# Chunk state update of a state-space layer: one fp32 product replaced by three passes over split operands

## The chip, the cores and the metric

The kernel runs on one core of one Trainium2 chip. The metric is the device time of one execution in microseconds (us). Three runs of the kernel before took 1937.16, 1936.15 and 1934.88 us; their median is 1936.15 us.

## What is computed

One decoder layer over 1024 positions of width 1024, in float32. `u = h @ w_in` feeds a Conformer branch (a gated unit, a causal depthwise convolution of 31 taps, a layer norm, a product), a Mamba-2 state-space branch and two gates; the gated sum goes through `w_o` and a layer norm, and a convolutional gated MLP follows. The change lies in the state-space branch. It works on chunks of 128 positions, for 4 groups of 8 heads (64 channels each) with a state of 128:

```python
xs = (x * dt[..., None])                       # positions x heads x channels
cb = jnp.einsum("bclgn,bcsgn->bcgls", cc, bc)
y_diag = jnp.einsum("bcgrls,bcsgrp->bclgrp", cb[:, :, :, None] * decay, xs)
decay_states = jnp.exp(a_cs[..., -1:] - a_cs)
states = jnp.einsum("bclgn,bcgrl,bclgrp->bcgrpn", bc, decay_states, xs)
...
    return d_c[..., None, None] * carry + s_c, carry     # scan over the chunks
...
y_off = jnp.einsum("bclgn,bcgrpn,bcgrl->bclgrp", cc, prev, jnp.exp(a_cs))
```

The product that the change touches is `states`: for one group and one chunk the transposed B (128 positions x 128 states) times the scaled x (128 positions x 512 channels).

## The kernel before

The sequence is worked in two halves of 512 positions, `mixers(0)` and `combine(0)`, then `mixers(1)` and `combine(1)`, then the MLP. Nearly all large products are made from operands that are split in two: a high part, the value rounded to the type `fp32r`, and a low part, the float32 value minus the high part. `mm3` (L187) then issues three TensorE passes of 128x512 into one bank of PSUM: high x high (L190), high x low (L191), low x high (L192). `project` (L194) calls it 8 times for a column block, so a block is 24 passes. ScalarE makes a weight's high part (L156), VectorE its low part (L161).

`mixers` runs over 4 groups. For each it projects columns, applies a convolution of 4 taps to B, C and x (`conv4`, L517), makes the gate (`z_gate`), the gated unit of two blocks of channels (`glu`, L540 to L542), then the chunks (`ssd_group`), and, at low priority, the 31 taps of two blocks of channels (`conv31`, L564), 30 VectorE instructions of 128x512 for each block. Per chunk `ssd_group` has on TensorE: 4 transposes of x and one of B (L614, L617), the product of B and C (L618), 8 small products with the masked decay `m` (L653), 8 with the carried state (L656, none in the first chunk) and, unless it is the last chunk of the sequence, the state product (L661). There are 16 chunks with a state product in the first half (4 groups x 4) and 12 in the second. On VectorE: the two scaled copies of x (L638, L643), the masked B and C product (L636), `m` times it (L648), the state update (L665, L668), the result (L671, L681). GpSimd multiplies `ce` by C (L632). The operands of the state product are plain float32: `xsd` (L643, read out of PSUM) and `bt` (L647, a ScalarE copy out of PSUM).

`combine` adds up the branches. The layer norm over the convolution's channels needs all 8 blocks: GpSimd sums them (L803), a product with a constant gives the mean (L808), VectorE subtracts (L810), ScalarE squares, GpSimd sums (L816), a second product (L820), a root and a reciprocal (L821, L822), a multiplication (L825), a SiLU (L826), and the split of the result `sT` (L206, L207). The products `w_co` of `sT` come after those of `w_gb` and `w_sp`, which do not need it.

The order on each engine is made when the program is built, by a scheduler that places instructions by priority and by what it takes to be ready. Each engine then works through its own list in order. SyncE issues most of the DMAs.

Of the kernel before, what the change touches and what calls it, by code (L numbers as in the profile page):

```python
# [8 lines left out]
F32 = mybir.dt.float32  # L9
F32R = mybir.dt.float32r  # L10
AF = mybir.ActivationFunctionType
ALU = mybir.AluOpType
# [4 lines left out]
P = 128  # L17
D = 1024
T = 1024
HALF = 512  # L20
# [41 lines left out]
def kernel(  # L62
# [124 lines left out]
    def mm3(ps, wa, xa, start, stop, more=False):  # L187


        TE.matmul(ps, wa(0), xa(0), start=start, stop=False, skip_group_check=more)  # L190
        TE.matmul(ps, wa(0), xa(1), start=False, stop=False, skip_group_check=more)  # L191
        TE.matmul(ps, wa(1), xa(0), start=False, stop=stop, skip_group_check=more)  # L192
# [337 lines left out]
    def glu(pl, hh, hT, i):  # L530
        pa, pg = bank(1), bank(1)
        wa = col_weights(hh, CT_A + i)
        project(pa, wa, hT)
        wg = col_weights(hh, CT_G + i)
        project(pg, wg, hT)
        v = (statep if i & 2 else pl).tile(
            [P, HALF + KC - 1], F32, tag="v", bufs=2, name=f"v{hh}_{i}"
        )
        s = pl.tile([P, HALF], F32, tag="sig", name=f"sig{hh}_{i}")
        A.activation(out=s, in_=pg, func=AF.Sigmoid)  # L540
        A.copy(v[:, : KC - 1], v_halo[:, i, :])
        V.tensor_mul(v[:, KC - 1 :], pa, s)  # L542
        if hh == 0:
            A.copy(v_halo[:, i, :], v[:, HALF:])
        return v
# [44 lines left out]
    def ssd_group(pl, hh, g, xT, BT, CT, zs):  # L590
        S = states[g]
        h8 = slice(8 * g, 8 * g + 8)

        def heads(t):
            return t.rearrange("p (h q) -> p h q", h=8)

        def per_head(t):
            return t.unsqueeze(2).to_broadcast([P, 8, HP])

        ssum = pl.tile([P, HALF], F32, tag="ssum", name=f"ssum{hh}_{g}")  # L600
        for c in range(4):
            nm = f"{hh}_{g}_{c}"
            cs = slice(c * P, (c + 1) * P)
            first = hh == 0 and c == 0
            last = hh == 1 and c == 3
            ab = pl.tile([P, 8, P], F32, tag="ab", name=f"ab{nm}")
            r = c * HEADS + 8 * g
            SY.dma_start(
                ab.rearrange("p h l -> p (h l)"),
                acs_scr[hh][r : r + 8, :].rearrange("h l -> (h l)").partition_broadcast(P),  # L610
            )
            px = bank(0)
            for i in range(4):
                TE.transpose(px[:, i * P : (i + 1) * P], xT[:, i, cs], ident)  # L614
            pb = bank(0)
            if not last:
                TE.transpose(pb[:, :P], BT[:, cs], ident)  # L617
            TE.matmul(pb[:, P : 2 * P], BT[:, cs], CT[:, cs], start=True, stop=True)  # L618
            m = pl.tile([P, 8, P], F32, tag="m", name=f"m{nm}")
            for h in range(8):  # L620
                A.activation(  # L621
                    out=m[:, h, :],
                    in_=ab[:, h, :],
                    func=AF.Relu,
                    scale=-1.0,
                    bias=acs[:, c, 8 * g + h : 8 * g + h + 1],
                )
            exps.append(A.activation(out=m, in_=m, func=AF.Exp, scale=-1.0))
            if not first:
                ce = pl.tile([P, 8, P], F32, tag="ce", name=f"ce{nm}")  # L630
                A.activation(out=ce, in_=ab, func=AF.Exp)  # L631
                G.tensor_tensor(  # L632
                    out=ce, in0=ce, in1=CT[:, cs].unsqueeze(1).to_broadcast([P, 8, P]), op=ALU.mult
                )
            cbm = pl.tile([P, P], F32, tag="cbm", name=f"cbm{nm}")
            V.tensor_mul(cbm, pb[:, P : 2 * P], upper)  # L636
            xs = pl.tile([P, HALF], F32, tag="xs", name=f"xs{nm}")
            V.tensor_tensor(  # L638
                out=heads(xs), in0=heads(px), in1=per_head(dts[0][:, c, h8]), op=ALU.mult
            )  # L640
            if not last:
                xsd = pl.tile([P, HALF], F32, tag="xsd", name=f"xsd{nm}")
                V.tensor_tensor(  # L643
                    out=heads(xsd), in0=heads(px), in1=per_head(dts[1][:, c, h8]), op=ALU.mult
                )
                bt = pl.tile([P, P], F32, tag="bt", name=f"bt{nm}")
                A.copy(bt, pb[:, :P])  # L647
            V.tensor_tensor(out=m, in0=m, in1=cbm.unsqueeze(1).to_broadcast([P, 8, P]), op=ALU.mult)  # L648
            py = bank(0)
            for i in range(4):  # L650
                pair = [(2 * i + k, py[k * HP : (k + 1) * HP, i * P : (i + 1) * P]) for k in (0, 1)]
                for h, o in pair:
                    TE.matmul(o, xs[:, h * HP : (h + 1) * HP], m[:, h, :], start=True, stop=first)  # L653
                if not first:
                    for h, o in pair:
                        TE.matmul(  # L656
                            o, S[:, h * HP : (h + 1) * HP], ce[:, h, :], start=False, stop=True
                        )
            if not last:
                pn = bank(0)  # L660
                TE.matmul(pn, bt, xsd, start=True, stop=True)  # L661
                if first:
                    V.tensor_copy(S, pn)
                else:
                    V.tensor_tensor(  # L665
                        out=heads(S), in0=heads(S), in1=per_head(edc[:, 1, c, h8]), op=ALU.mult
                    )
                    V.tensor_add(S, S, pn)  # L668
            for i in range(4):
                k = PC_SD + 4 * g + i  # L670
                skip = V.scalar_tensor_tensor(  # L671
                    out=xT[:, i, cs],
                    in0=xT[:, i, cs],
                    scalar=pc[:, k : k + 1],
                    in1=py[:, i * P : (i + 1) * P],
                    op0=ALU.mult,
                    op1=ALU.add,
                )
            while held and c == 0:
                issue_after(held.pop(), skip)  # L680
            V.tensor_mul(xT[:, :, cs], xT[:, :, cs], zs[:, :, cs])  # L681
            sq = pl.tile([P, 4, P], F32, tag="sq", name=f"sq{nm}")
            A.activation(out=sq, in_=xT[:, :, cs], func=AF.Square)
            V.tensor_add(sq[:, 0:2], sq[:, 0:2], sq[:, 2:4])
            V.tensor_add(ssum[:, cs], sq[:, 0], sq[:, 1])

        def scaled():
            rstd = pl.tile([P, HALF], F32, tag="rstd", name=f"rstd{hh}_{g}")
            rows = pl.tile([P, P], F32, tag="rows", name=f"rows{hh}_{g}")
            pv = bank(0)  # L690
            for j in range(4):
                TE.matmul(
                    pv[j * HEADS : (j + 1) * HEADS, :P],
                    ones[:, :HEADS],
                    ssum[:, j * P : (j + 1) * P],
                    start=True,
                    stop=True,
                    tile_position=(0, j * HEADS),
                )
            A.activation(out=rows, in_=pv[:, :P], func=AF.Sqrt, bias=eps, scale=1.0 / HALF)  # L700
            V.reciprocal(out=rows, in_=rows)
            scr = nrm_scr[hh * GROUPS + g]
            G.dma_start(scr, rows.rearrange("(j r) l -> j r l", j=4)[:, 0, :])
            G.dma_start(rstd, scr.rearrange("j l -> (j l)").partition_broadcast(P))
            for i in range(4):
                k = PC_NW + 4 * g + i
                by_row = V.scalar_tensor_tensor(
                    out=xT[:, i, :],
                    in0=xT[:, i, :],
                    scalar=pc[:, k : k + 1],  # L710
                    in1=rstd,
                    op0=ALU.mult,
                    op1=ALU.mult,
                )
                held.append(by_row)

        def parts(yT):
            ks = slice((g % 2) * 4, (g % 2) * 4 + 4)
            hi, lo = yT[:, 0, ks], yT[:, 1, ks]
            for n in (slice(0, 2), slice(2, 4)):  # L720
                A.copy(hi[:, n], xT[:, n])
                V.tensor_tensor(
                    out=lo[:, n], in0=xT[:, n], in1=hi[:, n].bitcast(F32), op=ALU.subtract
                )

        return scaled, parts
# [768 lines left out]
```

## Time and profile before

| of the profiled execution | |
|---|---|
| span | 1934.5 us (no other time of this execution is listed; the median of the runs is 1.6 us above it) |
| VectorE busy | 1600.7 us, 83% of the span |
| ScalarE busy | 1092.2 us, 56% |
| GpSimd busy | 216.7 us, 11% |
| share of the DMA engines, in the 40 slices | 0.3 to 0.7 |
| granted TensorE clock | 0.999 |
| state products L661 | 56 records (two for each of 28 products), from 108.1 to 1057.4 us |

The page gives busy time by engine, then the span in 40 slices, then the chain of work that ended last, then groups of instructions. A group of TensorE passes shows a mean of about 390 ns each, but the passes overlap: what one costs is read from the starts in the timeline, not from its duration. The same holds, less strongly, for VectorE.

### The profile page before, as it was taken

The numbers are of one execution on the slowest core, as the hardware profiler recorded it, in microseconds if no ns is written. First come the engines' busy times: TensorE is split into PE (matmuls) and PEld (weight loads), VectorE is DVE, ScalarE is ACT, GpSimd is POOL, SyncE is SP. The second block draws the span as 40 slices with busy tenths as digits, with TensorE's granted clock in tenths as the row PEclk, the third lists the DMA queues.
The fourth block names the chain that finished last, engine by engine and source line by source line (L and its number), as shares of the span: only waits on it lengthen the run. The fifth ranks groups of instructions, "written<-read, shape, count | busy, mean of one in ns | idle before, by whom it ended". The sixth has DMA issues, their size and how long they took to land.

```text
span 1934.5 us, 25807 instructions
## 1 busy us (share of the span) xinstructions
PE 1921.9 (99%) x9424; PEld 1570.4 (81%) x9424; DVE 1600.7 (83%) x2230; ACT 1092.2 (56%) x1641; POOL 216.7 (11%) x256
## 2 busy tenths in 40 slices
PE   9999999999999999999999999999999999999998
PEld 8888877788888788888888888888888888887886
DVE  7599999999897639899999546597788888888778
ACT  7576767753353366776765435365555555543544
POOL 1001010112300001111112140010000000122010
PEclk9999999999999999999999999999999999999999
DMA  6645555547456665656545644566455555479673
GB/s 231 219 169 200 172 201 185 167 160 267 135 183 228 207 208 176 211 177 211 177 162 166 219 143 135 182 241 225 163 171 185 178 185 185 161 276 355 198 250 115
DMA packets 127216, 376.27 MB, mean 195 GB/s; under 512 B 15184, under 2 KB 15728, under 8 KB 127088
## 3 DMA queue, kind: packets, MB, share of 16 engines
q1 hardware_dynamic: 107424, 318.48, 48.7%
q0 software_dynamic: 13184, 44.59, 6.5%
q10 hardware_dynamic: 6480, 11.55, 1.6%
q8 instruction: 74, 1.21, 0.3%
q14 instruction: 54, 0.44, 0.1%
HBM read 290.00 MB, written 84.56 MB: 194 GB/s over the span
## 4 chain that ended last, share of the span: by engine, by line
PE 86%; DVE 9%; DMA 3%; ACT 1%; issue 1%; SPq 0%; DVEq 0%; POOL 0%; ACTq 0%; POOLq 0%
PE acc L192 20%; PE acc L191 20%; PE acc L190 20%; PE sm L190 6%; PE sm L192 6%; PE sm L191 6%; DVE c L564 3%; DMA dr<-wdown 2%; PE sm L653 1%; PE sm L661 1%; PE sm L656 1%; DVE x L517 1%; PE acc L498 1%; DMA st_wo<-wo 1%; PE sm L614 1%
## 5 line engine op out<-in xcount | busy, mean ns | idle before, releaser
L192 PE MATMUL acc<-hT_h,w_c 128*128 128x512 f32 x1000 | 391.4, 392 | 0.0
L191 PE MATMUL acc<-hT_l,w_c 128*128 128x512 f32 x1000 | 391.1, 391 | 0.0
L190 PE MATMUL acc<-hT_h,w_c 128*128 128x512 f32 x1000 | 391.0, 391 | 0.0
L564 DVE SCALAR_TENSOR_TENSOR c<-v,pc,c 128x512 f32<-128x512 f32 x480 | 371.1, 798 | 7.0 <-ACT c L553 4.5
L190 PEld LDWEIGHTS acc<-hT_h,w_c 128*128 128x128 f32 x1000 | 187.8, 188 | 40.6 <-issue 1.9
L192 PEld LDWEIGHTS acc<-hT_h,w_c 128*128 128x128 f32 x1000 | 187.8, 188 | 40.4 <-issue 1.5
L191 PEld LDWEIGHTS acc<-hT_l,w_c 128*128 128x128 f32 x1000 | 187.8, 188 | 39.5 <-issue 1.1
L156 ACT CAST w_c<-st_c 128x1024 fp32r<-128x1024 f32 x128 | 133.8, 1046 | 111.4 <-PE acc L192 84.3
L632 POOL TENSOR_TENSOR ce<-ce,xbc 128x1024 f32<-128x1024 f32 x28 | 78.3, 2796 | 686.8 <-ACT ce L631 686.8
L1260 ACT CAST w_dn<-dr 128x1024 fp32r<-128x1024 f32 (+1 forms) x72 | 67.2, 942 | 76.7 <-DVE dr L1193 36.0
L190 PE MATMUL sm<-h1s,w_s 128*128 128x512 f32 x264 | 102.8, 389 | 0.5 <-ACT fuv L1103 0.5
L191 PE MATMUL sm<-h1s,w_s 128*128 128x512 f32 x264 | 102.7, 389 | 0.0
L192 PE MATMUL sm<-h1s,w_s 128*128 128x512 f32 x264 | 102.2, 389 | 0.0
L621 ACT ACTIVATE m<-ab,acs 128x128 f32<-128x128 f32 x256 | 78.4, 390 | 39.5 <-PE sm L653 37.8
L161 DVE TENSOR_TENSOR w_c<-st_c,w_c 128x1024 fp32r<-128x1024 f32 x62 | 76.7, 1237 | 17.5 <-ACT w_c L156 17.4
L1261 DVE TENSOR_TENSOR w_dn<-dr,w_dn 128x1024 fp32r<-128x1024 f32 (+1 forms) x72 | 77.6, 1084 | 6.3 <-ACT w_dn L1260 6.2
L517 DVE SCALAR_TENSOR_TENSOR x<-u,pc,x 128x512 f32<-128x512 f32 x96 | 78.0, 826 | 5.7 <-ACT x L515 5.6
L192 PE MATMUL acc<-h1b_h,w_ue 128*128 128x512 f32 x176 | 68.7, 395 | 0.3 <-DVE w_ue L161 0.3
L190 PE MATMUL acc<-h1b_h,w_ue 128*128 128x512 f32 x176 | 68.8, 391 | 0.0
L191 PE MATMUL acc<-h1b_l,w_ue 128*128 128x512 f32 x176 | 68.6, 390 | 0.0
L190 PE MATMUL sm<-h1b_h,w_s 128*128 128x512 f32 x176 | 68.5, 389 | 0.0
L191 PE MATMUL sm<-h1b_l,w_s 128*128 128x512 f32 x176 | 68.5, 389 | 0.0
(369 smaller groups left out, 4544.7 us busy)
## 6 DMA issues: line engine op xcount, KB each, us to landing
st_c<-wcol SPq DMA_DIRECT2D x128, 512.0 KB, 4.4
low_scr<-w_c SPq DMA_DIRECT2D x64, 512.0 KB, 2.9
w_c<-low_scr SPq DMA_DIRECT2D x64, 512.0 KB, 4.4
ab<-acs_scr SPq DMA_DIRECT2D x32, 512.0 KB, 4.2
dr<-wdown SPq DMA_DIRECT2D x55, 256.0 KB, 4.9
st_wo<-wo SPq DMA_DIRECT2D x24, 512.0 KB, 4.3
st_ue<-wup SPq DMA_DIRECT2D x22, 512.0 KB, 3.7
first_scr<-first ACTq DMA_DIRECT2D x44, 256.0 KB, 3.0
```

The lines of the kernel that those rows point to most:

```text
L156: casts.append(A.copy(w[:, 0, :], st))
L161: sub.tensor_tensor(out=w[:, 1, :], in0=st, in1=w[:, 0, :].bitcast(F32), op=ALU.subtract)
L190: TE.matmul(ps, wa(0), xa(0), start=start, stop=False, skip_group_check=more)
L191: TE.matmul(ps, wa(0), xa(1), start=False, stop=False, skip_group_check=more)
L192: TE.matmul(ps, wa(1), xa(0), start=False, stop=stop, skip_group_check=more)
L498: mm = TE.matmul(pss[o][:, ts], ws[o][:, i, k * P : (k + 1) * P], hT[:, j, k, ts], start=n == 0 and k == 0, stop=n == 2 and k == KD - 1,)
L517: V.scalar_tensor_tensor(out=o, in0=u[:, k : k + HALF], scalar=pc[:, wc + k : wc + k + 1], in1=o, op0=ALU.mult, op1=ALU.add,)
L564: V.scalar_tensor_tensor(out=accs[i], in0=v[:, k : k + HALF], scalar=pc[:, wc + k : wc + k + 1], in1=accs[i], op0=ALU.mult, op1=ALU.add,)
L621: A.activation(out=m[:, h, :], in_=ab[:, h, :], func=AF.Relu, scale=-1.0, bias=acs[:, c, 8 * g + h : 8 * g + h + 1],)
L632: G.tensor_tensor(out=ce, in0=ce, in1=CT[:, cs].unsqueeze(1).to_broadcast([P, 8, P]), op=ALU.mult)
L1260: A.copy(w[:, 0, cs], src)
L1261: V.tensor_tensor(out=w[:, 1, cs], in0=src, in1=w[:, 0, cs].bitcast(F32), op=ALU.subtract)
```

## The change

```diff
-        s = pl.tile([P, HALF], F32, tag="sig", name=f"sig{hh}_{i}")
+        s = pl.tile([P, HALF], F32, tag="ya", bufs=2, name=f"sig{hh}_{i}")
...
             if not last:
-                xsd = pl.tile([P, HALF], F32, tag="xsd", name=f"xsd{nm}")
+                xsd = pl.tile([P, 2, HALF], F32R, tag="xsd", name=f"xsd{nm}")
+                whole = pl.tile([P, HALF], F32, tag="whole", name=f"whole{nm}")
                 V.tensor_tensor(
-                    out=heads(xsd), in0=heads(px), in1=per_head(dts[1][:, c, h8]), op=ALU.mult
-                )
-                bt = pl.tile([P, P], F32, tag="bt", name=f"bt{nm}")
-                A.copy(bt, pb[:, :P])
+                    out=heads(whole), in0=heads(px), in1=per_head(dts[1][:, c, h8]), op=ALU.mult
+                )
+                bt = pl.tile([P, 2, P], F32R, tag="bt", name=f"bt{nm}")
+                for n, src in ((bt, pb[:, :P]), (xsd, whole)):
+                    A.copy(n[:, 0, :], src)
+                    V.tensor_tensor(
+                        out=n[:, 1, :], in0=src, in1=n[:, 0, :].bitcast(F32), op=ALU.subtract
+                    )
...
-                TE.matmul(pn, bt, xsd, start=True, stop=True)
+                mm3(pn, lambda i: bt[:, i, :], lambda i: xsd[:, i, :], True, True)
```

Both operands are split as everywhere else, and the state product becomes three `fp32r` passes. Per chunk the change adds one ScalarE cast of 128x512 (`bt`'s copy becomes a cast), two VectorE subtractions (128x512 with both inputs in SBUF, 128x128 with one in PSUM), and turns one TensorE product of two records into three passes. No DMA is added. The tile `sig` of the gated unit loses its own buffer and takes turns in the two buffers `ya` that the branch results and gates use. Behind L648 the lines of the changed kernel stand 5 higher.

The scheduler makes a new order from this. Three places matter below. The first is a chunk's state product on TensorE, here the second chunk of the last group in the first half (`bt0_3_1`; `sm` is a PSUM bank, `w_so` a weight). Before:

```order
L656 MATMUL sm127_3661<-ce0_3_1_3649,state3_108 64x128 x2
L661 MATMUL sm128_3678<-xsd0_3_1_3656,bt0_3_1_3658 128x512
L614 MATMUL sm129_3693<-ident_75,x4_0_3_3137 128x128 x4
L617 MATMUL sm130_3698<-ident_75,xbc0_19_3087 128x128
L618 MATMUL sm130_3698<-xbc0_23_3128,xbc0_19_3087 128x128
L190 MATMUL acc142_3985<-yT0_0_h_1916,w_so0_5_3982 128x512
```

Of the change, on the same engine at the same chunk:

```order
L661 MATMUL sm127_3743<-ce0_3_1_3727,state3_108 64x128 x2
L190 MATMUL sm128_3760<-xsd0_3_1_3734,bt0_3_1_3737 128x512
L191 MATMUL sm128_3760<-xsd0_3_1_3734,bt0_3_1_3737 128x512
L192 MATMUL sm128_3760<-xsd0_3_1_3734,bt0_3_1_3737 128x512
L614 MATMUL sm129_3777<-ident_75,x4_0_3_3209 128x128 x4
L617 MATMUL sm130_3782<-ident_75,xbc0_19_3159 128x128
```

The three passes stand where the one product stood, between the small products of the old state and the next chunk's transposes.

The second place is VectorE around the same chunk (`c0_4`, `c0_5` are taps of the long convolution, `w_so` a weight's low part). Before:

```order
L643 TENSOR_TENSOR xsd0_3_1_3656<-sm125_3631,wds_110 128x512
L636 TENSOR_TENSOR cbm0_3_1_3652<-sm126_3636,upper_83 128x128
L564 SCALAR_TENSOR_TENSOR c0_5_2991<-v0_5_2727,pc_99,c0_5_2991 128x512
L564 SCALAR_TENSOR_TENSOR c0_4_2989<-v0_4_2659,pc_99,c0_4_2989 128x512
L681 TENSOR_TENSOR x4_0_3_3137<-x4_0_3_3137,zs0_3_3298 128x4x128
L161 TENSOR_TENSOR w_so0_5_3982<-st_so0_5_3980,w_so0_5_3982 128x1024
L648 TENSOR_TENSOR m0_3_1_3639<-m0_3_1_3639,cbm0_3_1_3652 128x1024
L564 SCALAR_TENSOR_TENSOR c0_5_2991<-v0_5_2727,pc_99,c0_5_2991 128x512
```

Of the change, from the second scaled copy's end on:

```order
L686 TENSOR_TENSOR x4_0_3_3209<-x4_0_3_3209,zs0_3_3370 128x4x128
L564 SCALAR_TENSOR_TENSOR c0_5_3063<-v0_5_2775,pc_99,c0_5_3063 128x512
L650 TENSOR_TENSOR xsd0_3_1_3734<-whole0_3_1_3735,xsd0_3_1_3734 128x512
L653 TENSOR_TENSOR m0_3_1_3717<-m0_3_1_3717,cbm0_3_1_3730 128x1024
L161 TENSOR_TENSOR w_so0_5_4078<-st_so0_5_4076,w_so0_5_4078 128x1024
L650 TENSOR_TENSOR bt0_3_1_3737<-sm126_3714,bt0_3_1_3737 128x128
L564 SCALAR_TENSOR_TENSOR c0_4_3061<-v0_4_2707,pc_99,c0_4_3061 128x512
```

The subtractions (L650) stand next to the chunk's multiplication; taps of the convolution move behind them, so that the convolution ends later.

The third place is TensorE at the end of the first half's convolution branch, where the products of `sT` begin. Before (`w_sp0_7` is the last block that does not need `sT`):

```order
L192 MATMUL acc171_5029<-yT0_2_h_4079,w_sp0_7_5032 128x512
L190 MATMUL acc172_5065<-sT0_4862,w_co0_0_5068 128x512
L191 MATMUL acc172_5065<-sT0_4862,w_co0_0_5068 128x512
L192 MATMUL acc172_5065<-sT0_4862,w_co0_0_5068 128x512
L190 MATMUL acc172_5065<-sT0_4862,w_co0_0_5068 128x512
```

Of the change:

```order
L192 MATMUL acc171_5125<-yT0_2_h_4175,w_sp0_7_5128 128x512
L190 MATMUL acc172_5161<-sT0_4958,w_co0_0_5164 128x512
L190 MATMUL acc173_5197<-sT0_4958,w_co0_1_5200 128x512
L191 MATMUL acc172_5161<-sT0_4958,w_co0_0_5164 128x512
L192 MATMUL acc172_5161<-sT0_4958,w_co0_0_5164 128x512
L190 MATMUL acc172_5161<-sT0_4958,w_co0_0_5164 128x512
L191 MATMUL acc173_5197<-sT0_4958,w_co0_1_5200 128x512
```

Two blocks of `w_co` now take turns, three passes each. Ahead of this, the mean product L808 has moved from the end of block `w_sp0_2` to just before the last pass of `w_sp0_4` (three blocks and 23 passes later), and L820 from behind `w_sp0_4` to behind `w_gb0_7`, so that only 48 passes, not 120, stand between L820 and the first pass of `w_co`. In the second half both stand where they stood. In SyncE's list some stores of the convolution's results and some loads of the chunks' decay rows (L574, L608) change places with a weight's load or store; the MLP's order is the same on every engine.

## The prediction

> **What bounds the kernel now.** I read the page's head, its chain of work, the waits of TensorE, and then the busy time by stage.
>
> ```profile
> span 1934.5 us, 25807 instructions
> PE 1921.9 (99%) x9424; PEld 1570.4 (81%) x9424; DVE 1600.7 (83%) x2230; ACT 1092.2 (56%) x1641; POOL 216.7 (11%) x256
> ...
> PE 86%; DVE 9%; DMA 3%; ACT 1%; issue 1%; SPq 0%; DVEq 0%; POOL 0%; ACTq 0%; POOLq 0%
> ```
>
> TensorE is busy for all but 12.6 us of the span, and the chain is 86% TensorE. So TensorE's list sets the time, and every other engine matters only where it makes that list wait. Of the stages that the change touches, the longest wait of TensorE for VectorE is one row (what a row's brackets hold is its idle time and releaser):
>
> ```profile
> 982.82 0.44 PE L653 MATMUL sm<-m,xs 128*64 128x128 f32 x4 [0.60 <-DVE m L648]
> ```
>
> But VectorE has little room there. The windows show, for the first half's chunks, the layer norm behind them, and the second half's chunks, the stage's length and then each engine's busy time (PE, PEld, DVE, ACT, POOL):
>
> ```profile
> 107.00:510.00 403.00, 403.00 (x2133) 324.68 (x2133) 398.59 (x581) 257.50 (x432) 49.46 (x33) 1.00 0.54 186
> 510.00:562.00 52.00, 52.00 (x228) 42.35 (x226) 39.97 (x50) 33.62 (x46) 13.79 (x12) 1.00 0.49 167
> ...
> 736.00:1075.00 339.00, 338.40 (x1904) 274.51 (x1903) 324.32 (x509) 236.75 (x385) 47.24 (x21) 1.00 0.55 184
> ```
>
> VectorE idles 4.4 us in the first stage, 12.0 in the second, 14.7 in the third. It holds because most of its work, the long convolution, can be put off. That makes the question: what does TensorE save, and does the added VectorE work come out as a wait?
>
> **The product on TensorE.** I go by the starts in the timeline: a chunk now; the one place where small float32 products are followed by `fp32r` passes; one where passes are followed by transposes; and eight steps of the plain stream.
>
> ```profile
> 145.90 0.39 PE L656 MATMUL sm<-ce,state 128*64 128x128 f32 x4
> 146.22 1.13 PE L661 MATMUL sm<-xsd,bt 128*128 128x512 f32 x2
> 147.18 0.60 PE L614 MATMUL sm<-ident,x 128*128 128x128 f32 x4
> ...
> 797.91 0.39 PE L656 MATMUL sm<-ce,state 128*64 128x128 f32 x4
> 798.23 0.50 PE L191 MATMUL acc<-hT_l,w_c 128*128 128x512 f32 x1
> 798.56 0.40 PE L192 MATMUL acc<-hT_h,w_c 128*128 128x512 f32 x1
> 798.80 0.39 PE L190 MATMUL acc<-hT_h,w_c 128*128 128x512 f32 x1
> ...
> 96.03 0.40 PE L192 MATMUL acc<-hT_h,w_c 128*128 128x512 f32 x1
> 96.26 0.60 PE L614 MATMUL sm<-ident,x 128*128 128x128 f32 x4
> ...
> 560.18 0.39 PE L192 MATMUL acc<-yT_h,w_sp 128*128 128x512 f32 x1
> ...
> 562.00 0.39 PE L191 MATMUL acc<-sT,w_co 128*128 128x512 f32 x1
> ```
>
> A plain pass costs 1.82 / 8 = 0.2275 us. Now: the state product starts 0.32 us after the last group of L656 and holds TensorE for 147.18 - 146.22 = 0.96 us. Changed: the first pass also starts 0.32 us after L656 (797.91 to 798.23), costs 0.33 us (it follows float32 work), the second 0.24, the third 0.23 until the transposes: 0.80 us. **Saved: 0.16 us a chunk, 28 x 0.16 = 4.5 us.** In the first half's four last chunks no transposes follow, and the sum is the same within 0.02 us. The new order also breaks one more run of passes with four small products (L692); by the same rows entering and leaving costs about 0.1 us each more than a plain pass, so I add 0.3 us.
>
> The Trainium skill, FP8 and Floating Point Precision, TensorE Precision Notes, says that true float32 takes four passes through the array. The two records' 0.96 us agree: four plain passes are 0.91. By that rule alone the change saves one pass in four, 28 x 0.2275 = 6.4 us; the row at 798.23, with its dearer first pass, speaks for the smaller saving.
>
> **What is added.** For VectorE and ScalarE:
>
> ```profile
> 539.69 3.70 DVE L825 TENSOR_TENSOR cc<-cc,stats 128x512 f32<-128x512 f32 x6
> ...
> 152.89 0.28 DVE L636 TENSOR_TENSOR cbm<-sm,upper 128x128 f32<-128x128 f32 x1
> 153.09 1.50 DVE L517 SCALAR_TENSOR_TENSOR x<-u,pc,x 128x512 f32<-128x512 f32 x1
> ...
> 505.90 1.21 DVE L161 TENSOR_TENSOR w_gb<-st_gb,w_gb 128x1024 fp32r<-128x1024 f32 x1
> 507.03 1.21 DVE L161 TENSOR_TENSOR w_sp<-st_sp,w_sp 128x1024 fp32r<-128x1024 f32 x1
> ...
> L206 ACT CAST mixT_h<-mb 128x512 fp32r<-128x512 f32 x16 | 10.0, 623 | 13.4 <-DVE mb L874 13.4
> L540 ACT ACTIVATE sig<-acc 128x512 f32<-128x512 f32 x16 | 9.5, 597 | 0.1
> ACT w_c L156 <- PE acc L192: 84.3, 43, 5.5
> ```
>
> Six two-input instructions of 128x512 take 3.70 us, so one costs 0.60 from start to start (the last lasts 0.68); one of 128x128 costs 0.20; a weight's low part 1.13. The two subtractions thus cost VectorE 0.80 us a chunk: 12.8 us in the first half, 9.6 in the second, 22.4 in all. ScalarE gets 28 casts of about 0.6 us, 17 us; in the first stage it idles for 145 us, and its weight casts are early: they wait 43 times for TensorE to free a buffer. I cost them at nothing; should one stand too early in ScalarE's list, a weight cast queues behind it and TensorE waits for that, a few tenths each time. The new buffers of `sig` cost nothing: ScalarE idles 0.1 us in all before L540. SyncE's moved stores and loads each pass one weight transfer; I cost them at nothing too, with 0.2 us a place if the cover were gone.
>
> **Does the chunk wait for its operands?** One chunk, VectorE's `m` and TensorE's first product with it:
>
> ```profile
> 396.53 1.21 DVE L648 TENSOR_TENSOR m<-m,cbm 128x1024 f32<-128x1024 f32 x1
> ...
> 400.93 0.44 PE L653 MATMUL sm<-m,xs 128*64 128x128 f32 x4
> ```
>
> The margin is 400.93 - 397.74 = 3.2 us. I summed both lists, by such starts, up to this pair at all 16 chunks of the first half: the new order has VectorE between 2.5 us less and 2.9 us more ahead of `m`, TensorE between 2.2 less and 3.0 more ahead of L653, and the difference never eats more than 0.2 us of a margin. Taps were put behind the chunk in exchange for the splits. The low parts end at most 3.7 us behind `m`, the passes that need them start 1.2 to 2.2 us behind L653, so margins of 2 to 5 us cover them. In the second half the 9.6 us fall on 14.7 us of idle time, most of which is one wait that simply gets shorter:
>
> ```profile
> DVE v L542 <- ACT sig L540: 8.6, 2, 5.5
> ```
>
> I cost this at nothing; the 0.60 us wait at 982.82 may grow or go. **The put-off taps end later**, and here they meet a deadline, the mean over all channels. Last taps of the first half, GpSimd's last sum, the product:
>
> ```profile
> 502.45 1.54 DVE L564 SCALAR_TENSOR_TENSOR c<-v,pc,c 128x512 f32<-128x512 f32 x2
> 504.13 1.30 POOL L803 TENSOR_TENSOR stats<-stats,c 128x512 f32<-128x512 f32 x1 [10.09 <-DVE c L564]
> 510.38 1.02 PE L808 MATMUL sm<-stats,mean_w 128*128 128x512 f32 x2
> ```
>
> The margin is 510.38 - 505.43 = 4.95 us. In the new order VectorE has, ahead of the last tap, 16 splits (12.8), five more low parts (5.7) and six more two-input instructions (3.6): 22.1 us. TensorE has 95 more passes ahead of L808 (21.6) less the saving (2.6): 19.0 us. The margin shrinks to 4.95 + 19.0 - 22.1 = 1.9 us: no wait.
>
> Then the norm's chain, with only 48 passes to hide it instead of 120:
>
> ```profile
> 533.02 1.02 PE L820 MATMUL sm<-stats,mean_w 128*128 128x512 f32 x2
> 534.28 1.28 ACT L821 ACT_TABLE_LOAD   x1
> 535.58 0.69 ACT L821 ACTIVATE stats<-sm,eps 128x512 f32<-128x512 f32 x1
> 536.30 3.35 DVE L822 RECIPROCAL stats<-stats 128x512 f32<-128x512 f32 x1 [0.53 <-ACT stats L821]
> ```
>
> From L820 to the reciprocal are 3.3 us, of which a weight cast of 1.05 stands ahead of the table load; in the new order it is a sigmoid of 0.6 instead: 2.9. Then 3.35, eight multiplications (4.8), one more two-input instruction (0.6), a low part (1.1) and the first low part of `sT` (0.7): it is there 13.4 us after L820. TensorE comes to the pass that needs it after 0.5 for L820, 48 passes (10.9, and 0.4 more for the first, behind float32 work) and two high passes (0.5): 12.3. **A wait of 1.2 us**, between nothing and 4 if ScalarE's SiLUs come late as well. **The sum:** -4.5 + 0.3 + 1.2 = -3.0 us, a span of 1931.5; on the median of the runs **1933.1 us**.
>
> **The rivals.** (a) *Full saving*: the chain keeps up and the wait at 982.82 goes too: 1936.15 - 4.5 + 0.3 - 0.6 = 1931.3 us. For it: margins everywhere in the trace. Against: the two `w_co` blocks that take turns show a scheduler with nothing else left. If float32 costs are as the four-pass rule has them, 1929.8. (b) *VectorE falls behind*, slower. Place: the last tap of the first half, ahead of L808. Rows:
>
> ```profile
> 898.58 2.54 POOL L632 TENSOR_TENSOR ce<-ce,xbc 128x1024 f32<-128x1024 f32 x1 [11.25 <-ACT ce L631]
> ...
> 898.77 4.47 DVE L564 SCALAR_TENSOR_TENSOR c<-v,pc,c 128x512 f32<-128x512 f32 x3
> ```
>
> Beside a GpSimd instruction three taps took 4.47 us where three plain ones take about 2.0: 2.4 us lost. The new 128x512 subtraction reads two operands from SBUF, as taps do. If one in four of the first half's 16 splits is held so over what the taps lose already, that is 9.6 us; 1.9 are margin, 7.7 become waits: 1933.1 + 7.7 = 1940.8 us. It decides from 1.9 us of lateness, and makes the kernel slower by 0.2% from about 9. Against it: a held split takes the place of a held tap.
>
> The Trainium skill, SBUF — State Buffer, Who interferes with whom, says so too: a VectorE instruction with two SBUF inputs and a GpSimd one that reads SBUF lock each other out for a whole instruction. The row at 898.77 agrees.
>
> (c) *Nothing moves*: stray waits behind ScalarE's casts, some tenths at each of 28 chunks, eat the 3 us: about 1936.
>
> **How the numbers follow.** A measurement of this kernel tells about 0.2%, 3.9 us, from no change. The forecast and (c) stay within it: 0.45. (a), with the forecast's lower edge, is faster: 0.33, of which 0.05 for the four-pass figure. (b) is slower: 0.22. The range from 1929.5 (the largest saving) to 1940.5 (most of (b)) leaves out about 0.15.
>
> **What would show it.** Right: three passes of 0.80 us between L656 and L614; L653 with margins as now; L808 without a wait; one wait of 1 to 2 us at the first L191 of `sT`. Wrong: a wait of TensorE at L808 or at several chunks (b), a weight cast late behind `xsd`'s (c), or 0.2 us and more a chunk saved (a). The forecast also falls if the order costs time at a place where I summed nothing, such as `conv4` before the transposes.

## The result, and the profile after

The change makes the kernel slower. Four runs took 1944.15 to 1949.33 us, median **1945.94 us**, beside 1935.92 us for the kernel before on the same chip: a ratio of **1.0052, with a 95% interval of 1.0039 to 1.0065**, about 10 us. The forecast was 1933.1 us, 3 us faster, with a range from 1929.5 to 1940.5. One execution each of three experiments below (`h_late`, where it is the profiled one, `f2_after27`, `j_passes27`) was disturbed as a whole (2751 to 5621 us) and is left out.

The profiled execution of the changed kernel has a span of 1942.4 us, 7.9 us longer than the profile of before. Its page, head and chain of work:

```profile
span 1942.4 us, 25956 instructions
...
PE 1920.1 (99%) x9452; PEld 1575.8 (81%) x9452; DVE 1625.9 (84%) x2286; ACT 1102.8 (57%) x1666; POOL 216.8 (11%) x256
...
PE 72%; DVE 20%; DMA 3%; issue 2%; ACT 2%; DVEq 0%; POOL 0%; SPq 0%; ACTq 0%; POOLq 0%
```

TensorE is busy 1.8 us less than before (1921.9), but the span is longer: it idles 22 us instead of 13. In the chain VectorE's share has risen from 9% to 20% at TensorE's cost. VectorE's busy time grew by 25.2 us, about what the durations of its 56 added instructions come to (26.9). The rows of the waits view that name TensorE and that belong to the changed part (total, times, longest):

```profile
PE sm L658 <- DVE m L653: 5.2, 5, 1.7
PE acc L191 <- DVE sT L207: 2.1, 1, 2.1
PE sm L813 <- POOL stats L808: 2.0, 1, 2.0
...
PE acc L192 <- DVE w_sp L161: 1.4, 1, 1.4
...
PE acc L192 <- DVE w_gb L161: 0.4, 1, 0.4
```

Before, this list held one row, 0.6 us for `m`. (L653, L658, L808, L813 are the old L648, L653, L803, L808.) Now there are 11.1 us in nine waits, all made by VectorE: the sum `stats` that GpSimd hands over was itself waiting for VectorE's last tap. The product itself is not at fault. One chunk of the first half in TensorE's timeline:

```profile
149.61 0.39 PE L661 MATMUL sm<-ce,state 128*64 128x128 f32 x4
149.92 0.50 PE L190 MATMUL sm<-xsd,bt 128*128 128x512 f32 x1
150.26 0.39 PE L191 MATMUL sm<-xsd,bt 128*128 128x512 f32 x1
150.49 0.39 PE L192 MATMUL sm<-xsd,bt 128*128 128x512 f32 x1
150.72 0.60 PE L614 MATMUL sm<-ident,x 128*128 128x128 f32 x4
```

From 149.92 to 150.72 are 0.80 us in place of 0.96, exactly the price that was forecast. So 4.5 us were saved, and more than 12 lost. The loss in two stages, the windows of after (length, then busy time of PE, PEld, DVE, ACT, POOL, clock, DMA), and below the dots the one window of before that has not been shown:

```profile
510.00:562.00 52.00, 49.99 (x217) 40.42 (x216) 46.97 (x53) 20.44 (x28) 15.41 (x10) 1.00 0.40 140
562.00:600.00 38.00, 35.95 (x159) 29.14 (x158) 36.57 (x56) 20.63 (x32) 3.71 (x7) 0.96 0.56 196
736.00:1075.00 339.00, 334.38 (x1887) 275.06 (x1886) 326.24 (x514) 244.36 (x397) 48.27 (x21) 1.00 0.53 182
...
562.00:600.00 38.00, 38.00 (x169) 31.49 (x168) 33.52 (x47) 12.10 (x17) 2.13 (x4) 1.00 0.65 214
```

Before, TensorE was busy for all of the first two windows and VectorE idled 12 of the 52 us behind the first half's chunks; now VectorE idles 5 there, because taps that used to be over by 504 us still run. In the second half's chunks VectorE's idle time fell by only 1.9 us (14.7 to 12.8) though 9.6 us of work came in.

### The profile page after: what moved, and what is told of

It is laid out like the page before. It is cut to its first block, busy times and chain, and to the rows that moved or that the text cites. A ratio compares the mean times of both kernels' runs of the same rounds, so it can differ in the third digit from the quotient of the medians.

```text
span 1942.4 us, 25956 instructions
## 1 busy us (share of the span) xinstructions
PE 1920.1 (99%) x9452; PEld 1575.8 (81%) x9452; DVE 1625.9 (84%) x2286; ACT 1102.8 (57%) x1666; POOL 216.8 (11%) x256
## 4 chain that ended last, share of the span: by engine, by line
PE 72%; DVE 20%; DMA 3%; issue 2%; ACT 2%; DVEq 0%; POOL 0%; SPq 0%; ACTq 0%; POOLq 0%
PE acc L192 16%; PE acc L191 16%; PE acc L190 16%; DVE c L564 9%; PE sm L190 6%; PE sm L192 6%; PE sm L191 6%; DMA dr<-wdown 1%; PE acc L498 1%; PE sm L658 1%; DVE x L517 1%; DVE m L653 1%; DVE x L676 1%; DMA st_wo<-wo 1%; PE sm L661 1%
## 5 line engine op out<-in xcount | busy, mean ns | idle before, releaser
L191 PE MATMUL acc<-hT_l,w_c 128*128 128x512 f32 x1000 | 390.1, 390 | 0.0
L564 DVE SCALAR_TENSOR_TENSOR c<-v,pc,c 128x512 f32<-128x512 f32 x480 | 375.9, 808 | 9.1 <-ACT c L553 6.6
L191 PEld LDWEIGHTS acc<-hT_l,w_c 128*128 128x128 f32 x1000 | 187.8, 188 | 39.0 <-issue 0.5
L191 PE MATMUL sm<-h1s,w_s 128*128 128x512 f32 x264 | 102.7, 389 | 0.0
L517 DVE SCALAR_TENSOR_TENSOR x<-u,pc,x 128x512 f32<-128x512 f32 x96 | 72.9, 773 | 5.8 <-ACT x L515 5.7
L191 PE MATMUL acc<-h1b_l,w_ue 128*128 128x512 f32 x176 | 68.5, 389 | 0.0
L191 PE MATMUL sm<-h1b_l,w_s 128*128 128x512 f32 x176 | 68.5, 389 | 0.0
```

Of the source, the lines that this page charges most:

```text
L517: V.scalar_tensor_tensor(out=o, in0=u[:, k : k + HALF], scalar=pc[:, wc + k : wc + k + 1], in1=o, op0=ALU.mult, op1=ALU.add,)
L564: V.scalar_tensor_tensor(out=accs[i], in0=v[:, k : k + HALF], scalar=pc[:, wc + k : wc + k + 1], in1=accs[i], op0=ALU.mult, op1=ALU.add,)
```

## Experiments

Each kernel was timed against the kernel before on the same chip. "Ratio" is that of its times to those.

**Which part of the change costs the time?** The product's three passes alone, with the splits left out:

```diff
-                xsd = pl.tile([P, 2, HALF], F32R, tag="xsd", name=f"xsd{nm}")
-                whole = pl.tile([P, HALF], F32, tag="whole", name=f"whole{nm}")
+                xsd = pl.tile([P, HALF], F32R, tag="xsd", name=f"xsd{nm}")
...
-                bt = pl.tile([P, 2, P], F32R, tag="bt", name=f"bt{nm}")
-                for n, src in ((bt, pb[:, :P]), (xsd, whole)):
...
+                bt = pl.tile([P, P], F32R, tag="bt", name=f"bt{nm}")
+                A.copy(bt, pb[:, :P])
...
-                mm3(pn, lambda i: bt[:, i, :], lambda i: xsd[:, i, :], True, True)
+                mm3(pn, lambda i: bt, lambda i: xsd, True, True)
```

> Three passes from the high parts alone: the low parts, and with them the two subtractions, the tile whole and ScalarE's cast of it, are left out (VectorE writes the scaled x rounded), so VectorE and ScalarE do what they did before. If the added VectorE work (or ScalarE's casts) made the change slow: only TensorE's saving of 4.7 us is left, 1931.3 us (1930 to 1933), TensorE's gaps about 8 us as before. If the three passes themselves or the new buffers of sig upset the order: 1936 to 1942, with gaps of 12 us or more.

The splits alone, with the float32 product kept:

```diff
-                mm3(pn, lambda i: bt[:, i, :], lambda i: xsd[:, i, :], True, True)
+                TE.matmul(
+                    pn, bt[:, 0, :].bitcast(F32), xsd[:, 0, :].bitcast(F32), start=True, stop=True
+                )
```

> The cast, the tile whole and both subtractions as in the change, but one float32 product of the high parts (the low parts are made and not used). If the added work is the cause: the changed kernel's waits without TensorE's saving, 1946 + 4.7 = 1950.6 us (1945 to 1954), with waits of TensorE on VectorE of some 8 us or more. If the passes are the cause: 1936 (within 2).

The passes with ScalarE's cast of `whole`, without the subtractions:

```diff
                 for n, src in ((bt, pb[:, :P]), (xsd, whole)):
-                    A.copy(n[:, 0, :], src)
-                    V.tensor_tensor(
-                        out=n[:, 1, :], in0=src, in1=n[:, 0, :].bitcast(F32), op=ALU.subtract
-                    )
+                    A.copy(n, src)
```

> Three passes of the high parts, with the tile whole and ScalarE's cast of it, without the two subtractions (the low parts are left out): VectorE's work is that of before. If VectorE's load is the cause: within 1.5 us of the run with passes alone, 1931 to 1933. If ScalarE's cast, standing in order behind VectorE's multiplication, is the cause: 1941 to 1946, and the row of ScalarE's xsd waiting for whole near the 29.9 us of the changed kernel.

And the kernel before with only `sig` moved to the buffers `ya`:

```diff
-        s = pl.tile([P, HALF], F32, tag="sig", name=f"sig{hh}_{i}")
+        s = pl.tile([P, HALF], F32, tag="ya", bufs=2, name=f"sig{hh}_{i}")
```

> The kernel before with only the new buffers of sig (sig takes turns in the two buffers ya). If VectorE's load is the cause: nothing, 1936 to 1938. If the buffers make ScalarE wait or upset the order: 1940 or more.

| run | median us | ratio | 95% interval |
|---|---|---|---|
| e2_passes | 1937.74 | 1.0002 | 0.9994 to 1.0011 |
| e3_work | 1948.91 | 1.0054 | 1.0041 to 1.0068 |
| e4_casts | 1938.39 | 1.0005 | 0.9997 to 1.0014 |
| e1_tag | 1936.57 | 1.0000 | 0.9991 to 1.0009 |

The splits by themselves cost 10.5 us (e3), and without the subtractions nothing is lost (e2, e4), so the two subtractions on VectorE are the cause; neither the casts nor the buffers are. A second finding was not expected: the passes alone bring nothing either (e2 and e4 both miss the 1930 to 1933 us that were forecast for them), though the 4.5 us are saved at the product. Most of them come back as waits. Rows of TensorE's waits in e2, where VectorE has exactly the work of the kernel before:

```profile
PE sm L653 <- DVE m L648: 2.2, 3, 1.1
...
PE acc L192 <- DVE w_so L161: 1.1, 1, 1.1
...
PE sm L808 <- POOL stats L803: 0.7, 1, 0.7
```

That is 4.0 us, against 0.6 before. When TensorE becomes faster it runs into VectorE, so VectorE nearly paces these stages already in the kernel before.

**Is it VectorE's sum of work?** The long convolution is the bulk of it, so leaving out its first taps gives VectorE room: 4 taps in every block take 42 us off it, 2 taps 21 us, about what the splits add.

```diff
-        for k in range(KC - 1):
+        for k in range(4, KC - 1):
```

Run on the kernel before (f1_before27), on the changed kernel (f2_after27; with 2 in place of 4, f3_after29), and on the kernel of e2 (j_passes27).

> The kernel before with the first 4 of the 31 taps left out in every block (64 VectorE instructions of some 0.65 us, 42 us of VectorE's work). If VectorE's room is what the change uses up: little to win here, since only 0.6 us of TensorE's waits in this part were VectorE's: 1935 to 1937. It is the yardstick for the next two. If VectorE already paces the kernel before: 1930 or less.

> The changed kernel with the same 4 taps left out: VectorE has 42 - 22 = 20 us less to do than in the kernel before. If the cause is VectorE's load: TensorE's saving of 4.7 us comes out, 4 to 5 us below the kernel before with 27 taps, so 1930 to 1932.5. If the passes, ScalarE's casts or the buffers of sig are the cause: 6 us or more above it, 1941 to 1946.

> The changed kernel with the first 2 taps left out (21 us of VectorE's work, against the 22 that the splits add): VectorE's sum is that of the kernel before and of the run with passes alone. If VectorE's load is the cause: 1936 to 1939, as the run with passes alone (1937.7). If it is not: 1943 to 1947.

> The three passes alone (low parts left out) and the first 4 taps left out in every block: VectorE has 42 us less to do, and neither it nor ScalarE has any work of the split. If TensorE's saving is real and was only swallowed by VectorE's pace: 4 to 5 us below the kernel before with 27 taps (0.9996), 0.997 to 0.998, 1931 to 1932.5. If the saving is not there: 0.999 to 1.0.

| run | median us | ratio | 95% interval |
|---|---|---|---|
| f1_before27 | 1936.15 | 0.9996 | 0.9987 to 1.0004 |
| f2_after27 | 1935.94 | 0.9991 | 0.9982 to 1.0000 |
| f3_after29 | 1936.87 | 1.0002 | 0.9993 to 1.0011 |
| j_passes27 | 1932.12 | 0.9979 | 0.9970 to 0.9988 |

f3 puts VectorE back where it was, and the whole loss is gone: the same 1.0002 as the passes alone. With room for VectorE and no splits (j) the passes are 0.17% below f1, 3.3 us of the 4.5; the two intervals just touch. In the kernel before, room for VectorE by itself brings nothing that can be told (f1). f2 missed its number: its ratio cannot be told from f1's. Its trace has no wait for VectorE left in these stages, but two for ScalarE, 1.4 and 0.3 us. ScalarE and TensorE at the longer one:

```profile
349.22 0.62 ACT L649 CAST xsd<-whole 128x512 fp32r<-128x512 f32 x1
349.73 0.28 ACT L649 CAST bt<-sm 128x128 fp32r<-128x128 f32 x1
349.88 1.06 ACT L156 CAST w_c<-st_c 128x1024 fp32r<-128x1024 f32 x1
...
351.00 0.50 PE L190 MATMUL acc<-hT_h,w_c 128*128 128x512 f32 x1 [1.38 <-ACT w_c L156]
```

The new cast of `xsd` stands ahead of the weight's cast in ScalarE's list and TensorE waits 1.38 us. This is the prediction's rival (c); e3's trace has a wait of the same kind, 0.9 us at 163 us. It can account for a part of what f2 lacks, not for all. Some of the rest goes with the clock: f2's four executions with a granted clock of 0.999, the profiled one among them, took 1932.7 to 1934.0 us, its six with 0.998 took 1935.6 to 1937.0. What brought the clock down in those six was not profiled, and even the four miss the forecast, so the rest stays open. f3 too has one wait for ScalarE (2.0 us, for `x` at L515); ahead of that `x` stand old instructions (`m`, a table load, `ce`), no new cast.

**Which subtraction?** One operand split and the other only rounded, still three passes:

```diff
-                for n, src in ((bt, pb[:, :P]), (xsd, whole)):
+                for n, src in ((bt, pb[:, :P]),):
...
-                mm3(pn, lambda i: bt[:, i, :], lambda i: xsd[:, i, :], True, True)
+                mm3(pn, lambda i: bt[:, i, :], lambda i: xsd, True, True)
```

and the reverse for `xsd`.

> Three passes with bt split and xsd rounded (xsd's low part, ScalarE's cast of it and the tile whole are left out): VectorE gets 28 x 0.20 = 5.6 us instead of 22.4. If VectorE's load is the cause, in proportion: 1937.7 of the passes alone plus a quarter of 8 us, 1938 to 1941. If any split upsets the order: 1943 to 1947.

> Three passes with xsd split and bt rounded (bt's low part is left out): VectorE gets 28 x 0.60 = 16.8 us, three quarters of 22.4, ScalarE the cast. If VectorE runs out of room somewhere between 5.6 and 16.8 us: 1941 to 1945, nearly the whole loss. If each subtraction costs in proportion: 1941 to 1942 too, but then bt's alone should have cost 2; if the loss needs both: under 1939.

`bt` alone (5.6 us more for VectorE): 1934.72 us, ratio 0.9988 (0.9979 to 0.9997). `xsd` alone (16.8 us): 1944.21 us, 1.0043 (1.0029 to 1.0056). The loss is not in proportion: the first 5.6 us cost nothing, and somewhere up to 16.8 VectorE runs out of room. That `bt` alone comes out 0.1% below e2, where 2 us above it was expected, also says how far a new order by itself moves the time; differences of that size are not explained here.

**In which half?** The split and the passes in one half of the sequence, the float32 product in the other (the operands are made by the same condition):

```diff
...
+                if hh == 0:
                     mm3(pn, lambda i: bt[:, i, :], lambda i: xsd[:, i, :], True, True)
+                else:
+                    TE.matmul(pn, bt, xsd, start=True, stop=True)
```

> The split and the three passes in the first half alone (16 products), the float32 product in the second half (12). If each half pays for its own VectorE work: TensorE's waits of the first half (6.5 us at four places in the changed kernel) less the saving of 2.6, so 3 to 5 us above the kernel before, 1940 to 1942, and the waits at the chunks of the second half's last group gone. If the order alone is the cause: no such division, 1936 or 1946.

> The split and the three passes in the second half alone (12 products), float32 in the first half. The first half alone measured 1.0035 of the kernel before, 6.8 us, the whole change about 9 to 10. If the halves add up: 2 to 4 us over the kernel before, with the waits of TensorE on VectorE's m in the last two groups (some 5 us) as in the changed kernel and none at the mean product of the first half. If not: near 1937 or over 1943.

First half alone: 1943.68 us, 1.0035 (1.0021 to 1.0048), above its 1940 to 1942. Second half alone: 1940.18 us, 1.0015 (1.0006 to 1.0024). Together 1.0050, the whole change 1.0052: the halves add up. The traces divide as expected, f4 with the waits at `w_sp`, `stats` and `sT`, g_second with the same 5.2 us at `m` as the whole change.

**Sum or order in the second half?** VectorE at the second chunk of the last group, in the changed kernel:

```profile
1042.12 0.27 DVE L636 TENSOR_TENSOR cbm<-sm,upper 128x128 f32<-128x128 f32 x1
1042.32 0.73 DVE L564 SCALAR_TENSOR_TENSOR c<-v,pc,c 128x512 f32<-128x512 f32 x1
1042.98 0.67 DVE L673 TENSOR_TENSOR state<-state,sm 128x512 f32<-128x512 f32 x1
1043.58 0.68 DVE L686 TENSOR_TENSOR x<-x,zs 128x512 f32<-128x512 f32 x1
1044.18 0.74 DVE L564 SCALAR_TENSOR_TENSOR c<-v,pc,c 128x512 f32<-128x512 f32 x1
1044.84 1.21 DVE L161 TENSOR_TENSOR w_so<-st_so,w_so 128x1024 fp32r<-128x1024 f32 x1
1045.98 1.21 DVE L653 TENSOR_TENSOR m<-m,cbm 128x1024 f32<-128x1024 f32 x1
...
1047.33 0.44 PE L658 MATMUL sm<-m,xs 128*64 128x128 f32 x4 [1.31 <-DVE m L653]
```

Two taps stand between `cbm` and the `m` that TensorE is waiting for, and more stand ahead of those. These taps have time: the second half's last tap starts at 1096.9 us and the sums of it on GpSimd at 1129.5. So I held taps of the last group back until the chunks' `m` had been issued, by an order rule without a wait:

```diff
+                for c, n in enumerate((2, 6, 10, 15)):
+                    if hh and i > 5 and k == n:
+                        issue_after(tap, products[-4 + c])
```

(`products` lists the instructions of `m`.) It ran on the whole change, twice, and on the kernel with the second half alone.

> The changed kernel, with taps of the long convolution in the last group of the second half put behind the chunks' m in VectorE's list (7, 8, 10 and 14 taps further back at the four chunks); no work is added or left out. If the waits there come of the list's order (taps ahead of what TensorE waits for, with 30 us of room at the taps' own deadline): the three waits at 1045, 1064 and 1080 us go, 3 to 4.5 us less than the changed kernel, 1941 to 1943. If VectorE's sum of work alone sets the end: the time is lost again at the second half's mean product or norm, 1945 to 1947.

> The kernel of the run with the taps of the last group further back, once more for its trace. Order: the waits at m of the last group gone, 1941 to 1943.5. Sum of work: as the changed kernel, 1945 to 1947, with a new wait at the second half's mean product or norm.

> The split in the second half alone, and the taps of its last group further back. Order: the three waits of 3.7 us go, 1.0015 of the kernel before becomes 0.999 to 1.0, 1935.5 to 1937.5. Sum of work: 1.001 to 1.002 as without.

Whole change: 1944.86 us, 1.0038 (1.0024 to 1.0052), and 1944.48 us, 1.0041 (1.0029 to 1.0054), against 1.0052. Second half alone: 1936.26 us, 1.0002 (0.9993 to 1.0011), against 1.0015. Each lies 2 to 3 us lower, but the intervals overlap, and both times of the whole change fall between what order (1941 to 1943.5) and sum of work (1945 to 1947) were expected to give. So the times of the whole change do not decide, and the waits have to: those of h_late_b, and below the dots the `m` row of g_late.

```profile
PE sm L819 <- POOL stats L814: 2.1, 1, 2.1
PE acc L191 <- DVE sT L207: 2.1, 1, 2.1
PE sm L664 <- DVE m L656: 1.7, 1, 1.7
...
PE sm L672 <- DVE m L664: 1.7, 1, 1.7
```

Of five waits for `m` (5.2 us) the one that ends at 990 us, ahead of the taps that were moved, is left; the others are gone, and no new wait of the second half's norm has come for them. The order was the cause there. The first half's waits for `stats`, `sT` and `w_gb` stay; that for `w_sp` (1.4) is gone. That the whole change gained so little is partly the clock: h_late_b's profiled execution has one slow stretch more than the changed kernel's (last section), some 1.7 us.

Order acts in two ways here, and these runs do not part them. One is taps ahead of `m` in the list. The other is which instruction meets GpSimd. A row of the changed kernel's VectorE, and GpSimd's at the time:

```profile
1033.16 2.89 DVE L564 SCALAR_TENSOR_TENSOR c<-v,pc,c 128x512 f32<-128x512 f32 x1
...
1032.97 2.52 POOL L632 TENSOR_TENSOR ce<-ce,xbc 128x1024 f32<-128x1024 f32 x1 [5.90 <-ACT ce L631]
```

A tap that elsewhere takes 0.74 us took 2.89 beside GpSimd's multiplication. In the changed kernel three taps behind 1025 us are held so (at 1033, 1054 and 1074 us, 5.4 us more than three plain ones), in h_late_b and g_late one (1.0 us); in the kernel before none is behind 991 us.

**Could GpSimd take the work?**

```diff
-                for n, src in ((bt, pb[:, :P]), (xsd, whole)):
+                for n, src, eng in ((bt, pb[:, :P], V), (xsd, whole, G)):
                     A.copy(n[:, 0, :], src)
-                    V.tensor_tensor(
+                    eng.tensor_tensor(
```

> The whole change, but GpSimd makes xsd's low part (28 subtractions of 128x512, some 1.3 us each by its sums of the same size): VectorE is spared 28 x 0.60 = 16.8 of the 22.4 us. If VectorE's load is the cause: most waits of TensorE go, 1932 to 1937. If ScalarE's cast is the cause: 1943 to 1947, as the changed kernel. If GpSimd and VectorE hold each other up: over 1946, VectorE's mean tap well above 808 ns.

1958.01 us, 1.0104 (1.0091 to 1.0118): twice the loss. The subtraction's row in the view of its line (least, median and most ns behind the colon), and the taps' row in the groups (busy us and mean ns behind the first bar):

```profile
L650 POOL TENSOR_TENSOR xsd<-whole,xsd x28: 1288/1746/4012, 100.3 to 1069.4; 128x512 fp32r<-128x512 f32 x28
```

```profile
L564 DVE SCALAR_TENSOR_TENSOR c<-v,pc,c 128x512 f32<-128x512 f32 x480 | 390.1, 836 | 8.7 <-ACT c L553 6.0
```

Here the two engines do hold each other up: the mean tap rises from 808 to 836 ns, over 480 taps 13 us (nearly all of it on 25 of them, see the last section), and GpSimd takes up to 4.0 us for what it can do in 1.3. VectorE's busy time, 1634.0 us, is higher than in the changed kernel although 19 us of work were taken away.

None of these versions that computes the whole result is told apart from the kernel before on the fast side (`bt` alone is, by 0.12%, but it leaves out `xsd`'s low part).

## Why the prediction was wrong, step by step

- **TensorE's saving** was right as a price: 0.80 against 0.96 us a chunk, with the dearer first pass (0.34). The four-pass figure of 6.4 us was not borne out. (With that figure rival (a) comes to 1929.5 us, the range's lower edge; its 1929.8 leaves out the 0.3 and the 0.6.) As a term of the time, -4.5 us in full, it failed: e2, where VectorE has no added work, measured 1.0002.
- **VectorE's added work** was right as a sum (22.4 us by starts) and so was the place of the danger, the last tap ahead of the mean product. The step that failed there is the **margin of 1.9 us at L808**. TensorE's side held: without its waits it came 19.3 us later than before, against 19.0. VectorE's side did not: from the end of the first `m` (102.5 before, 103.1 after) to the end of the last tap it took 401.5 us before and 430.0 after, 28.5 more in place of 22.1. The last taps, the sum and the product in the changed kernel:

```profile
531.61 1.53 DVE L564 SCALAR_TENSOR_TENSOR c<-v,pc,c 128x512 f32<-128x512 f32 x2
533.28 1.27 POOL L808 TENSOR_TENSOR stats<-stats,c 128x512 f32<-128x512 f32 x1 [6.72 <-DVE c L564]
534.60 1.12 PE L813 MATMUL sm<-stats,mean_w 128*128 128x512 f32 x2 [2.01 <-POOL stats L808]
```

  The 6.4 us that were missed are idle time of VectorE ahead of that tap. Its waits up to there, of after:

```profile
DVE x L712 <- DMA rstd<-nrm_scr: 3.7, 1, 3.7
DVE c L564 <- ACT c L553: 2.1, 1, 2.1
DVE w_c L161 <- ACT w_c L156: 1.5, 1, 1.5
DVE sq L689 <- ACT sq L688: 1.3, 1, 1.3
DVE w_so L161 <- ACT w_so L156: 1.1, 1, 1.1
```

  They make 9.7 us; before there was one row, 2.4 us, for `yT_l`: 7.3 more, which covers the 6.4. I had added up instructions and taken VectorE's list as gapless. In the new order an instruction that needs a transfer (`rstd`) or ScalarE stands where its operand is not there yet, and everything behind it stands still.
- **The second half "costed at nothing"** was wrong, and the premise with it: the 9.6 us should have fallen on 14.7 us of idle time. Most of that idle is the wait for `sig`, which hangs on TensorE's own products and lies ahead of the later chunks. It shrank from 8.6 to 4.4 us, no more, and could not be filled afterwards. From the first to the last `m` of the half VectorE took 326.4 us before and 335.0 after. To the new work came hold-ups beside GpSimd: the taps and `conv4` steps of the half that took over 0.95 us lost 14.6 us against plain ones before, 18.3 after. The chunks' margins, which I had worked out for all 16 chunks of the first half, I did not work out here; in the last group they fell from 3.9 to 4.8 us to 0.15.
- **The margins of the first half's chunks** held: the first small product still stands 2.3 us or more behind `m` at all 16. (One shrank by 1.3 us, from 4.6 to 3.3, where the sum allowed 0.2.) But the room that was kept there is room for `m` alone. A weight's low part that came late (`w_sp`, 1.4 us, `w_gb`, 0.4) was in no ledger.
- **The wait of 1.2 us at the first L191 of `sT`** came, at 2.1, and with a cost behind it that no step had (below). The reciprocal began 3.8 us after its product, not 2.9: a weight's cast (1.05 us) and a sigmoid both stood ahead of the table load.
- **Rival (b)** had the place and nearly the time (1940.8) with the wrong mechanism. All 28 new 128x512 subtractions took 675 to 690 ns, so none was held by GpSimd; ahead of L808 VectorE was late by its work and its waits. In the second half GpSimd did hold taps, as said above.
- **Rival (a)**, a chain that keeps up, had a third of the chance. e2 shows that it was not to be had even without the splits: TensorE at 99% and the chain at 86% do not say that the others would follow if TensorE went faster.

In sum, over the starts in the timeline: 4.5 us saved, and 0.3 for the extra break at the sum of squares. The places where TensorE's next instruction comes over 0.12 us later than the median for such a pair add up to 19.0 us after and 7.1 before (leaving out four slow first passes behind the old product, 1.6 us, which belong to its price, and the small products of L464, alike in both): 11.9 more, 1.6 of them in slow passes behind the wait for `sT` and 0.7 at a wait in the first norm, which the change does not touch. That makes 7.7 of the 7.9 us of the span. The median of the runs is 1.8 us above the profiled execution; what differs in the others was not profiled.

## What to carry to other kernels

An engine at 83% can be as binding as one at 99%: before moving work onto it, find its deadlines (here the last tap ahead of the mean) and count its waits as well as its instructions, since idle time that waits for the busy engine may not be there to be filled (here 9.6 us of work came on 14.7 of idle, and 1.9 of it was used). A saving on the busiest engine is worth only what the next one lets through; leaving work out on that next engine (some taps) shows it in one run. Where a list is fixed when the program is built, look for work with a late deadline that stands ahead of work somebody waits for; an order rule alone took four waits away here, and three hold-ups beside GpSimd became one.

## What the runs showed of the hardware

A wait of TensorE can cost more than its length. Behind the wait for `sT` in the changed kernel the passes go on at half speed for a while:

```profile
566.62 0.49 PE L191 MATMUL acc<-sT,w_co 128*128 128x512 f32 x1 [2.05 <-DVE sT L207]
566.95 0.39 PE L192 MATMUL acc<-sT,w_co 128*128 128x512 f32 x1
...
568.13 0.63 PE L191 MATMUL acc<-sT,w_co 128*128 128x512 f32 x1
568.55 0.63 PE L192 MATMUL acc<-sT,w_co 128*128 128x512 f32 x1
568.98 0.63 PE L190 MATMUL acc<-sT,w_co 128*128 128x512 f32 x1
...
571.11 0.57 PE L192 MATMUL acc<-sT,w_co 128*128 128x512 f32 x1
571.52 0.40 PE L190 MATMUL acc<-sT,w_co 128*128 128x512 f32 x1
```

From about 568 to 571.5 us a pass costs 0.43 us instead of 0.2275, 1.7 us in all. The granted clock of 562 to 600 us is 0.96 in the windows above. In h_late_b it happens at both long waits. A wait of the same length did not always do it: in the changed kernel the one that ends at 534.6 us (2.01) left the clock at 1.00, in h_late_b the one that ends at 533.2 (2.06) brought it down, in f3 one of 2.00 did. The waits of under 2 us at `m` in the changed kernel never did.

The traces tell why. The clock's changes in them fall on a grid of 3.413 us. Windows of the changed kernel on that grid, around both waits (length, TensorE's busy time first, the granted clock third from the end):

```profile
564.66:568.07 3.41, 1.45 (x6) 1.24 (x7) 3.41 (x6) 3.41 (x7) 1.05 (x2) 1.00 0.51 168
568.07:571.49 3.42, 3.42 (x9) 2.65 (x8) 3.42 (x6) 3.42 (x7) 0.53 (x1) 0.50 0.86 311
...
530.53:533.94 3.41, 2.06 (x10) 1.37 (x8) 2.57 (x4) 0.77 (x2) 0.66 (x1) 1.00 0.51 172
533.94:537.35 3.41, 2.75 (x10) 1.97 (x11) 2.85 (x4) 2.20 (x4) 0.61 (x1) 1.00 0.29 88
```

The wait for `sT` lies with 1.96 of its 2.05 us in one window, and the next window runs at 0.50. The wait for `stats` is cut in two by a border, 1.35 and 0.66 us, and nothing happens. In the 17 undisturbed traces, from the first change of the clock to 1920 us, all nine windows in which TensorE idled 1.96 us or more, by the ends that the profile gives, are followed by one at half clock, and none of those in which it idled 1.86 us or less. So it is the idle time within one window that counts. Where the borders lie differs from execution to execution: the first change of the clock came 4.6 to 7.8 us after the span's start.

The Trainium skill, TensorE: Matmul & The Clock Gate, What's actually happening, describes a clock that falls to half after an idle window of about 3.4 us and windows that run freely. The half speed, the 3.4 us that it lasts and the free windows agree; here a window that was idle for 1.96 of its 3.41 us was enough.

The second finding is the GpSimd run: the Trainium skill, SBUF — State Buffer, Who interferes with whom, says that a VectorE instruction with two SBUF inputs contends with a GpSimd instruction that reads SBUF. The trace agrees: the 25 taps that ran beside one of GpSimd's new subtractions took 1339 ns on average, the other 455 took 808. That is 13 of the 27 us by which VectorE's busy time came out above the changed kernel's less the 19 us taken away, so it is a good part of why that work came back.
